# Where attention's projection tiles are read out of PSUM, one weight split further ahead, the first tokens in halves, and a last norm in three pieces

## The chip, the core and the metric

The kernel runs on one core of one Trainium2 chip. The core has a matrix engine (TensorE, PE in the profile), three engines for elementwise work (VectorE as DVE, ScalarE as ACT, GpSimd as POOL), and SyncE (SP), which here only issues transfers. Each engine runs its own instructions strictly in the order in which they were laid down; between engines they wait for each other by semaphores. Matmul results land in PSUM, everything else lives in SBUF, and inputs, weights and outputs are in HBM. The metric is the device time of one execution in microseconds (us), as the median of several runs.

## The reference, cut to what matters

One layer of a decoder for 512 prompt tokens and 64 sample tokens (8 requests of 8 tokens), all in float32, width 1024, 16 query heads of 64 in 4 groups, feed-forward width 2816:

```
h = x @ w_in                                  # u | v | q | k | attn v | gate_A | gate_B
u = gelu(u);  va = layer_norm(gelu(v))
y_A = u * (tril(W_s) va_chunk + b_s)          # chunks of 128 tokens
y_B = sliding window (128) attention with a position bias and one sink logit per head
mix = (sigmoid(g_a) * (y_A @ w_pa) + sigmoid(g_b) * (y_B @ w_pb)) @ w_o
x = layer_norm(alpha * x + mix)
x = layer_norm(alpha * x + (silu(x @ w_gate) * (x @ w_up)) @ w_down)
```

The outputs are both groups' x, the last 128 key and value rows of each, and the sample's normalised v.

## The kernel before

**Number format.** Every float32 operand of a matmul is split into a rounded part "hi" and a remainder "lo" (`split`: a ScalarE copy writes hi, a VectorE subtraction writes lo), and a product is three matmuls: hi·hi, hi·lo, lo·hi. This holds for the weights too. They come in units of 128x1024 numbers: `fetch` issues the transfer of a unit on SP's queue into one of 3 buffers ("raw"), `convert` splits it into one of 4 pairs of buffers ("hi", "lo", lines 114 and 115), and `unit(a, ahead=1)` hands out the next unit after it has made sure that the unit `ahead` places behind it has been split as well.

**Order.** The program is written once, in order. A planner lays down each engine's instructions before the run: among those that it takes to be ready, by its own estimate of times, it takes the one written first, and otherwise one written later. So an engine's order can differ from the written one, and buffers can be filled well ahead. `tc.issue_after(ins)` pins what a block writes for the engine of `ins` behind `ins` in that engine's order; for other engines it says nothing.

**The start.** Ten warming matmuls run on zeros. Meanwhile ScalarE's queue issues the transfer of the first eighth of x (feature block k = 0, `xT[:, 0]`), and SP's queue issues weight unit 0 in two halves, x for k = 1, two small bias inputs, x for k = 2 and 3, unit 1, x for k = 4 to 7, unit 2. In `projections_and_attention` a loop over the 8 feature blocks k splits x (576 tokens at once) and multiplies it with units 0 and 1 into two tiles ("ps").

**Attention.** There are 16 blocks, (group g, 128 tokens n). Block i has these steps, and TensorE has them in this order: `attention_turn` transposes the probabilities of block i ("pT"; ScalarE and VectorE split them into "pt", GpSimd masks them into "pc" and "pt"); `attention_values` multiplies those of block i - 1 with the values ("po"; ScalarE copies the lower half to "bot", VectorE adds it into yB); `attention_scores` makes the scores of block i + 2 ("sc"; then ScalarE's copy to "work", and on VectorE the mask at line 573, the bias at 575, the maximum at 579, two small operations at 582 and 583, then four exponentials on ScalarE at 585, and on VectorE the normalisation at 588 to 590); then `column_tile` fills TensorE's time with one tile of the projection w_in, 48 matmuls, in the order of `FILLS`: q3 u0 k1 q4 q5 u1 q6 q7 u2 ... u7 g0 g1. A finished tile is read out of PSUM by `evac_q` (ScalarE lines 491 and 494, VectorE 496 and 501), `evac_k` (ScalarE 471, VectorE 476, ScalarE 479) or, for u and g, by one ScalarE copy (line 813). For q and k tiles this is written in the next block, just before that block's scores; for u and g tiles at once after the matmuls. Scores and projection tiles share three PSUM buffers in turn, so that the scores of block i + 2 take the buffer of the projection tile of block i - 2. Instead of scores, block 14 has those of the sample tokens ("pss", softmax in "samS", lines 657 to 672); their probabilities are transposed ("pst", line 686) after the last block, in PSUM that the projection tiles give back.

**After attention** come the gMLP's v projection ("acc_v", eight weight units, the first four in a loop over n), gates, the merge, the output projection and the feed-forward. The kernel ends with `last_norm` on the last 128 tokens: VectorE's means, two small GpSimd operations for the reciprocal deviation r (`rstd`, lines 325 and 326), VectorE's first pass (z - mean) * g over 1024 columns (line 1341), and then z * r + b in three column ranges on VectorE, ScalarE and GpSimd, each sent out by its own transfer.

Of the kernel before, what the change touches and what calls it, by code (L numbers as in the profile page):

```python
# [11 lines left out]
F32 = mybir.dt.float32  # L12
# [3 lines left out]
ALU = mybir.AluOpType  # L16
AX = mybir.AxisListType

P = 128
D = 1024  # L20
KC = D // P
NP = 512
NS = 64
NT = NP + NS
HB = NT // 2
# [51 lines left out]
class Builder:  # L77
# [284 lines left out]
    def build(self):  # L362
        psum = lambda name, bufs: self.tc.tile_pool(
            name=name, bufs=bufs, space=bass.MemoryType.PSUM, reuse_waits="tile")
        with psum("pp0", 3) as self.pp, psum("pb0", 2) as self.pb:
            self.first_loads()
            self.constants()
            self.projections_and_attention()
        with psum("pb", 8) as self.pb:
            self.sample_first()  # L370
            self.gmlp()
            self.merge()
            self.output_projection()
            self.ffn()
            self.ffn_down()
# [19 lines left out]
        for _ in range(10):  # L395
            self.mm(ps, z[:, :P], z[:], True, True)

    def first_loads(self):
        self.xraw2 = [self.C([2, NT], F32, f"xraw{i}") for i in range(4)]
        self.nc.scalar.dma_start(out=self.xraw2[0][:, 0], in_=self.I["xT"][:, 0])  # L400
        self.fetch(0, parts=2)

    def load_x(self):
        nc, xT = self.nc, self.I["xT"]
        r = self.xraw2
        self.xraw = [r[k // 2][:, k % 2] for k in range(KC)]
        nc.sync.dma_start(out=r[0][:, 1], in_=xT[:, 1])
        self.bias_lookup()
        nc.sync.dma_start(out=r[1][:], in_=xT[:, 2:4])
        self.fetch(1)  # L410
        nc.sync.dma_start(out=r[2][:], in_=xT[:, 4:6])
        nc.sync.dma_start(out=r[3][:], in_=xT[:, 6:8])
        self.fetch(2)
# [138 lines left out]
    def attention_scores(self, g, n):  # L552


        nc = self.nc
        q0 = n * P
        sc = self.PS(f"sc{g}_{n}")
        for r in range(4):
            q = self.qs[2 * g + r // 2][:, r % 2, q0 : q0 + P]
            s = slice(q0 - P if n else 0, q0 + P if n else 2 * P)  # L560
            o = sc[:, r // 2, 256 * (r % 2) : 256 * (r % 2) + 256]
            self.mm(o, q, self.kt[g][:, 0, s], True, False)
            self.mm(o, q, self.kt[g][:, 1, s], False, True)
        scv = sc.rearrange("p b (h k) -> p (b h) k", h=2)
        work = self.R([2, 4, P], F32, f"work{g}_{n}")
        sel, pr = work[:, 0], work[:, 1]
        if n:
            nc.scalar.copy(out=sel, in_=scv[:, :, :P])
            cur = scv[:, :, P:]
        else:  # L570
            nc.gpsimd.memset(sel, NEG)
            cur = scv[:, :, :P]
        nc.vector.copy_predicated(
            out=sel, mask=self.cmask.unsqueeze(1).to_broadcast([P, 4, P]), data=cur)
        nc.vector.tensor_tensor(
            out=sel, in0=sel, in1=self.Bsel[g // 2][:, 4 * (g % 2) : 4 * (g % 2) + 4], op=ALU.add)
        st = self.ST(16, "att")
        nm, rs, es, rec = (st[:, 4 * i : 4 * i + 4] for i in range(4))
        nc.vector.tensor_reduce(out=nm, in_=sel, axis=AX.X, op=ALU.max, negate=True)
        sg = self.sinks[:, 4 * g : 4 * g + 4]  # L580
        nsg = self.nsinks[:, 4 * g : 4 * g + 4]
        nc.vector.tensor_tensor(out=nm, in0=nm, in1=nsg, op=ALU.min)  # L582
        nc.vector.tensor_tensor(out=es, in0=nm, in1=sg, op=ALU.add)
        for r in range(4):
            nc.scalar.activation(  # L585
                out=pr[:, r], in_=sel[:, r], func=AF.Exp, bias=nm[:, r : r + 1], accum_out=rs[:, r : r + 1])
        nc.scalar.activation(out=es, in_=es, func=AF.Exp)
        nc.vector.tensor_tensor(out=rs, in0=rs, in1=es, op=ALU.add)
        nc.vector.reciprocal(out=rec, in_=rs)
        nc.vector.tensor_tensor(  # L590
            out=pr, in0=pr, in1=rec.unsqueeze(2).to_broadcast([P, 4, P]), op=ALU.mult)
        return pr
# [21 lines left out]
    def attention_values(self, g, n, parts):  # L614
        nc = self.nc
        po = self.bank(f"po{g}_{n}")
        q0 = n * P
        mms = [(blk, m[:, i]) for m, blk in parts for i in range(2)]
        for j, (blk, m) in enumerate(mms):
            self.mm(po, self.av[blk // 2][:, blk % 2, g], m, j == 0, j == len(mms) - 1)  # L620
        bot = self.SG(f"bot{g}_{n}")
        nc.scalar.copy(out=bot[:HD, :512], in_=po[HD:])
        for i in range(2):
            f = lambda a: a.rearrange("p (c i q) -> p c i q", c=2, i=2)[:, :, i]
            nc.vector.tensor_tensor(
                out=self.yB[g][HD * i : HD * i + HD, :, q0 : q0 + P],
                in0=f(po[:HD]), in1=f(bot[:HD, :512]), op=ALU.add)
# [88 lines left out]
    def projections_and_attention(self):  # L716
# [11 lines left out]
        for k in range(KC):  # L728
            if k % 4 == 0:
                u = self.unit(4, parts=4, ahead=0)  # L730
            self.split(self.X[:, k, :NT], self.X[:, k, NT:], self.xraw[k])
            xh, xl = self.xact(k)
            for c in range(2):
                wh, wl = (w[:, k % 4, P * c : P * c + P] for w in u)
                for b in range(2):
                    s = slice(b * HB, (b + 1) * HB)
                    o = tiles[c][:, b, :HB]
                    self.mm(o, wh, xh[:, s], k == 0, False)
                    self.mm(o, wh, xl[:, s], False, False)
                    self.mm(o, wl, xh[:, s], False, k == KC - 1)  # L740
            if k == 1:
                self.bias_products()
# [17 lines left out]
        for i, (g, n) in enumerate(blocks):  # L760
            if n == 0:
                self.yB.append(self.C([2, NT], F32, f"yB{g}"))
            turned = self.attention_turn(g, n, probs[i])
            if i:
                with self.tc.issue_after(self.last_turned.ins):
                    self.attention_values(*waiting)
                self.run(fill)
            if i + 2 < len(blocks):
                probs.append(self.attention_scores(*blocks[i + 2]))
                if i + 4 == len(blocks):  # L770
                    with self.tc.issue_after(self.selected.ins):
                        kc, vc = self.sample_keys()
            elif i + 1 < len(blocks):
                S = self.sample_scores(kc)
            waiting = g, n, turned
            fill = self.column_tile(*fills[i])
            with self.tc.issue_after(self.copied.ins) if i + 2 == len(blocks) else nullcontext():
                next(fill, None)
            if i + 1 == len(blocks):
                with self.tc.issue_after(self.last_mm.ins):  # L780
                    self.attention_values(*waiting)
            next(fill, None)
            if fills[i][0] not in "qk":
                self.run(fill)
        self.run(fill)
        self.sample = S, vc
# [7 lines left out]
        for _ in gen:  # L794
            pass

    def column_tile(self, kind, c):

        ps = self.PS(f"ps{kind}{c}")
        u = self.unit(KC)  # L800
        self.fm(ps, u, self.xact, ks=range(7))
        yield
        self.fm(ps, u, self.xact, ks=range(7, KC))
        yield
        if kind == "k":
            self.evac_k(ps, c)
        elif kind == "q":
            self.evac_q(ps, c)
        else:
            tiles = self.u if kind == "u" else self.T  # L810
            if c % 2 == 0:
                tiles.append(self.C([2, NT], F32, f"{kind}{c}"))
            self.copied = self.nc.scalar.copy(
                out=tiles[c // 2][:, c % 2].rearrange("p (b c) -> p b c", b=2), in_=ps[:, :, :HB])
# [27 lines left out]
    def gmlp(self):  # L842
# [41 lines left out]
        norm = lambda t: self.norm_steps(st[t], v[t], rows[t], lng, lnb)  # L884
        acc = self.accumulators("v0")
        for n in range(4):
            u = {n: self.unit(2)}
            for t in range(NB + 1):
                tile(t, acc[t], u, (2 * n, 2 * n + 1))
            if n == 0:  # L890
# [443 lines left out]
    def last_norm(self, st, z, g, b, dst):  # L1334
# [3 lines left out]
        r = self.ST(1, "lnr")  # L1338
        nc.vector.bn_aggr(out=mv[:], in_=st.rearrange("p (a b) -> p a b", a=3))
        self.rstd(mv, r, P)  # L1340
        nc.vector.scalar_tensor_tensor(
            out=z[:], in0=z[:], scalar=mv[:, 0:1], in1=g[:], op0=ALU.subtract, op1=ALU.mult)
        c = slice(832, D)
        nc.scalar.activation(out=z[:, c], in_=z[:, c], func=AF.Copy, scale=r[:])
        nc.gpsimd.tensor_tensor(out=z[:, c], in0=z[:, c], in1=b[:, c], op=ALU.add)
        for k, queue in ((slice(0, 416), nc.scalar), (slice(416, 832), nc.sync)):
            nc.vector.scalar_tensor_tensor(
                out=z[:, k], in0=z[:, k], scalar=r[:], in1=b[:, k], op0=ALU.mult, op1=ALU.add)
            sent = queue.dma_start(out=dst[:, k], in_=z[:, k])
# [112 lines left out]
```

## Time and profile before

| | us |
|---|---|
| median of 3 runs | 891.38 (891.34 to 892.84) |
| the profiled execution, its own time | 893.83 |
| span of the profiled execution | 892.1 |
| TensorE's matmuls busy | 876.7 (98%) |
| VectorE busy | 630.5 (71%) |
| ScalarE busy | 404.0 (45%) |
| GpSimd busy | 193.0 (22%) |

The span runs from the first to the last recorded instruction or transfer of one execution; its own time has 1.7 us around that. Times in the trace count from the span's start. A busy time is the union of an engine's instructions; the ends of matmuls are modelled. "Idle before" is the time in which the engine stood still before an instruction, and the arrow names what ended it.

### The profile page before, as it was taken

The numbers are of one execution on the slowest core, as the hardware profiler recorded it, in microseconds if no ns is written. First come the engines' busy times: TensorE is split into PE (matmuls) and PEld (weight loads), VectorE is DVE, ScalarE is ACT, GpSimd is POOL, SyncE is SP. The second block draws the span as 40 slices with busy tenths as digits, with TensorE's granted clock in tenths as the row PEclk, the third lists the DMA queues.
The fourth block names the chain that finished last, engine by engine and source line by source line (L and its number), as shares of the span: only waits on it lengthen the run. The fifth ranks groups of instructions, "written<-read, shape, count | busy, mean of one in ns | idle before, by whom it ended". The sixth has DMA issues, their size and how long they took to land.

```text
span 892.1 us, 14718 instructions
## 1 busy us (share of the span) xinstructions
PE 876.7 (98%) x5911; PEld 822.5 (92%) x5911; DVE 630.5 (71%) x931; ACT 404.0 (45%) x767; POOL 193.0 (22%) x205
## 2 busy tenths in 40 slices
PE   8999999989999999999999999999999999999996
PEld 7999999978899999999988999999999998888885
DVE  5778887744789788867777777777777779224236
ACT  6556565573354446324342444444444457111110
POOL 3012214222332112233402222222222220000003
PEclk9999999989999999999999999999999999999999
DMA  9432124164123215233560022223222225322202
GB/s 326 125 98 71 49 62 153 44 200 126 46 71 117 95 48 186 93 117 107 175 229 24 1 72 95 95 96 95 95 96 95 95 95 189 96 71 95 71 4 103
DMA packets 31024, 91.85 MB, mean 103 GB/s; under 512 B 3947, under 2 KB 9100, under 8 KB 30924
## 3 DMA queue, kind: packets, MB, share of 16 engines
q1 hardware_dynamic: 30620, 88.45, 29.9%
q10 hardware_dynamic: 336, 2.47, 0.7%
q8 instruction: 46, 0.75, 0.3%
q14 instruction: 22, 0.18, 0.1%
HBM read 86.77 MB, written 6.10 MB: 104 GB/s over the span
## 4 chain that ended last, share of the span: by engine, by line
PE 88%; DVE 6%; ACT 3%; issue 1%; POOL 1%; DMA 0%; DVEq 0%; ACTq 0%; POOLq 0%
PE d L295 16%; PE xf L295 14%; PE zf L295 7%; PE acc_v L295 6%; PE acc_o L295 6%; PE pspa L295 6%; PE xg L295 5%; PE psu L295 4%; PE yf L295 4%; PE ffn L295 3%; PE zg L295 3%; PE xp L295 2%; PE psq L295 2%; PE psav L295 2%; PE ps L295 1%
## 5 line engine op out<-in xcount | busy, mean ns | idle before, releaser
L115 DVE TENSOR_TENSOR lo<-raw,hi 128x1024 fp32r<-128x1024 f32 (+1 forms) x78 | 90.4, 1169 | 99.5 <-ACT hi L114 99.1
L115 DVE TENSOR_TENSOR glo<-raw,ghi 128x1024 fp32r<-128x1024 f32 (+1 forms) x93 | 100.7, 1086 | 55.3 <-ACT ghi L114 55.3
L295 PE MATMUL d<-hi,h 128*128 128x512 f32 (+1 forms) x440 | 128.0, 368 | 0.0
L114 ACT CAST hi<-raw 128x1024 fp32r<-128x1024 f32 (+1 forms) x78 | 75.7, 985 | 109.6 <-PE d L295 82.6
L114 ACT CAST ghi<-raw 128x1024 fp32r<-128x1024 f32 (+1 forms) x93 | 83.4, 900 | 58.5 <-DVE raw L177 53.9
L295 PEld LDWEIGHTS d<-hi,h 128*128 128x128 f32 x440 | 79.9, 189 | 13.7
L295 PE MATMUL d<-lo,h 128*128 128x512 f32 (+1 forms) x242 | 89.6, 370 | 0.0
L177 POOL TENSOR_TENSOR raw<-raw,t 128x512 f32<-128x512 f32 x31 | 40.7, 1312 | 197.9 <-DVE glo L115 145.4
L177 POOL TENSOR_TENSOR t<-raw,raw 128x512 f32<-128x512 f32 x31 | 43.0, 1388 | 115.6 <-DVE raw L177 115.6
L295 PE MATMUL xf<-x1T,ghi 128*128 128x288 f32 x320 | 65.0, 295 | 0.0
L115 DVE TENSOR_TENSOR glo<-t,ghi 128x1024 fp32r<-128x1024 f32 x31 | 64.5, 2081 | 0.0
L295 PEld LDWEIGHTS d<-lo,h 128*128 128x128 f32 x242 | 45.6, 188 | 7.8
L295 PEld LDWEIGHTS xf<-x1T,ghi 128*128 128x128 f32 x320 | 51.4, 188 | 0.2 <-DVE u L226 0.2
L325 POOL TENSOR_SCALAR lnr<-lnmv 128x1 f32<-128x1 f32 (+1 forms) x15 | 14.2, 944 | 169.7 <-DVE lnmv L343 166.4
L295 PE MATMUL xf<-x1T,glo 128*128 128x288 f32 x160 | 47.1, 294 | 0.0
L295 PE MATMUL acc_o<-hi,m 128*128 128x512 f32 x144 | 46.3, 391 | 0.0
L295 PE MATMUL pspa<-yA,hi 128*128 128x288 f32 x256 | 44.6, 294 | 0.3 <-DVE yA L115 0.3
L585 ACT ACTIVATE work<-work,att 128x128 f32<-128x128 f32 x64 | 25.0, 392 | 43.1 <-DVE att L582 42.9
L295 PE MATMUL psu<-X,hi 128*128 128x288 f32 x256 | 44.1, 294 | 0.0
L609 POOL TENSOR_SCALAR_AFFINE_SELECT pc<-pt 128x512 fp32r<-128x512 f32 x24 | 16.6, 690 | 126.5 <-ACT pt L114 125.4
L295 PE MATMUL acc_v<-hi,X 128*128 128x512 f32 x128 | 42.9, 401 | 0.0
L295 PE MATMUL psq<-X,hi 128*128 128x288 f32 x224 | 38.8, 294 | 0.0
(366 smaller groups left out, 2478.7 us busy)
## 6 DMA issues: line engine op xcount, KB each, us to landing
raw<-in_wall_dram SPq DMA_DIRECT2D x133, 512.0 KB
xr<-in_xT_dram SPq DMA_DIRECT2D x8, 288.0 KB
z<-in_xtok_dram SPq DMA_DIRECT2D x4, 512.0 KB
xraw<-in_xT_dram SPq DMA_DIRECT2D x3, 576.0 KB
out_y_prompt_dram<-z SPq DMA_DIRECT2D x3, 512.0 KB
circ<-bout SPq DMA_DIRECT2D x1, 1024.0 KB
Bsel<-circ SPq DMA_DIRECT2D x2, 512.0 KB
kc<-in_kcT_dram SPq DMA_DIRECT2D x2, 512.0 KB
```

The lines of the kernel that those rows point to most:

```text
L114: self.nc.scalar.copy(out=hi, in_=src)
L115: return self.nc.vector.tensor_tensor(out=lo, in0=src, in1=hi.bitcast(F32), op=ALU.subtract)
L177: sub = lambda e, out, x, y: e.tensor_tensor(out=out, in0=x, in1=y, op=ALU.subtract)
L295: self.last_mm = self.nc.tensor.matmul(out, l, r, start=start, stop=stop, **more)
L325: self.nc.gpsimd.tensor_scalar_add(r[:n], mv[:n, 1:2], EPS)
L585: nc.scalar.activation(out=pr[:, r], in_=sel[:, r], func=AF.Exp, bias=nm[:, r : r + 1], accum_out=rs[:, r : r + 1])
L609: self.selected = nc.gpsimd.affine_select(out=f(out[:, i]), in_=f(pt[:, i].bitcast(F32)), pattern=[[0, 4], [sign, P]], compare_op=cmp, fil ...
```

## The change

Six edits. (a) The projection tile of block i - 1 is read out after the scores of block i + 2 are written, pinned on ScalarE behind this block's "bot" copy (`self.lower`, line 622) and on VectorE behind its line 583 (`self.shifted`). (b) The u and g tiles are read there too, except u7, which is still read at once. (c) In block 14 (tile g0) weights are split two units ahead and not one, and that split is no longer pinned behind u7's copy. (d) In the gMLP's first four steps ScalarE's part of the weight splits is pinned behind the last projection tile's copy (`self.copied`, here g1's). (e) At the start all loads go out on SP's queue, unit 0 in pieces of 256, 256 and 512 columns with x for k = 0 and k = 1 between them, and x for k = 0 is split in two halves of 288 tokens. (f) The last norm's first pass is done in three pieces of 192, 416 and 416 columns.

```
@@ build
-            self.first_loads()
@@ 
-    def first_loads(self):
-        self.xraw2 = [self.C([2, NT], F32, f"xraw{i}") for i in range(4)]
-        self.nc.scalar.dma_start(out=self.xraw2[0][:, 0], in_=self.I["xT"][:, 0])
-        self.fetch(0, parts=2)
-
     def load_x(self):
         nc, xT = self.nc, self.I["xT"]
-        r = self.xraw2
+        r = [self.C([2, NT], F32, f"xraw{i}") for i in range(4)]
         self.xraw = [r[k // 2][:, k % 2] for k in range(KC)]
-        nc.sync.dma_start(out=r[0][:, 1], in_=xT[:, 1])
+        raw = self.praw.tile([P, 1024], F32, tag="raw", name="raw0")
+        self.raws.append(raw)
+        for c0, c1, k in ((0, 256, 0), (256, 512, 1), (512, 1024, None)):
+            nc.sync.dma_start(out=raw[:, c0:c1], in_=self.I["wall"][0][:, c0:c1])
+            if k is not None:
+                nc.sync.dma_start(out=r[0][:, k], in_=xT[:, k])
         self.bias_lookup()
@@ attention_scores
-        nc.vector.tensor_tensor(out=es, in0=nm, in1=sg, op=ALU.add)
+        self.shifted = nc.vector.tensor_tensor(out=es, in0=nm, in1=sg, op=ALU.add)
@@ attention_values
-        nc.scalar.copy(out=bot[:HD, :512], in_=po[HD:])
+        self.lower = nc.scalar.copy(out=bot[:HD, :512], in_=po[HD:])
@@ projections_and_attention
-            self.split(self.X[:, k, :NT], self.X[:, k, NT:], self.xraw[k])
+            for t0, t1 in ((0, HB), (HB, NT)) if k == 0 else ((0, NT),):
+                self.split(self.X[:, k, t0:t1], self.X[:, k, NT + t0 : NT + t1], self.xraw[k][:, t0:t1])
...
                     self.attention_values(*waiting)
-                self.run(fill)
             if i + 2 < len(blocks):
                 probs.append(self.attention_scores(*blocks[i + 2]))
...
+            if i:
+                with self.tc.issue_after(self.lower.ins), self.tc.issue_after(self.shifted.ins):
+                    self.run(fill)
             waiting = g, n, turned
-            fill = self.column_tile(*fills[i])
-            with self.tc.issue_after(self.copied.ins) if i + 2 == len(blocks) else nullcontext():
-                next(fill, None)
+            before_last = i + 2 == len(blocks)
+            fill = self.column_tile(*fills[i], ahead=1 + before_last)
+            next(fill, None)
...
-            if fills[i][0] not in "qk":
+            if i + 3 == len(blocks):
                 self.run(fill)
@@ column_tile
-    def column_tile(self, kind, c):
+    def column_tile(self, kind, c, ahead=1):
-        u = self.unit(KC)
+        u = self.unit(KC, ahead=ahead)
@@ gmlp
         for n in range(4):
-            u = {n: self.unit(2)}
+            with self.tc.issue_after(self.copied.ins):
+                u = {n: self.unit(2)}
@@ last_norm
-        nc.vector.scalar_tensor_tensor(
-            out=z[:], in0=z[:], scalar=mv[:, 0:1], in1=g[:], op0=ALU.subtract, op1=ALU.mult)
-        c = slice(832, D)
+        c0, c1, c = slice(0, 416), slice(416, 832), slice(832, D)
+        for k in (c, c0, c1):
+            nc.vector.scalar_tensor_tensor(
+                out=z[:, k], in0=z[:, k], scalar=mv[:, 0:1], in1=g[:, k], op0=ALU.subtract, op1=ALU.mult)
...
-        for k, queue in ((slice(0, 416), nc.scalar), (slice(416, 832), nc.sync)):
+        for k, queue in ((c0, nc.scalar), (c1, nc.sync)):
```

## Rows read from the trace of the kernel before

**Rows 1.** The page's first part, the row of TensorE: PE is its matmuls, PEld its weight loads; busy time, share of the span, instructions.
```profile
PE 876.7 (98%) x5911; PEld 822.5 (92%) x5911; DVE 630.5 (71%) x931; ACT 404.0 (45%) x767; POOL 193.0 (22%) x205
```

**Rows 2.** Who TensorE's matmuls waited for over the whole span: total us, times, longest.
```profile
PE pst L686 <- ACT g L813: 1.6, 1, 1.6
...
PE sc L295 <- DVE Z L501: 1.5, 2, 1.0
...
PE po L295 <- POOL pt L609: 1.1, 1, 1.1
```

**Rows 3.** Busy time by stretch: the stretch and its length, then busy us and count of PE, PEld, DVE, ACT, POOL, then the granted clock as a share of full speed, the DMA share and GB/s.
```profile
120.00:140.00 20.00, 18.91 (x140) 17.99 (x139) 15.35 (x34) 13.87 (x43) 2.65 (x5) 1.00 0.25 77
...
190.00:195.00 5.00, 5.00 (x17) 4.29 (x18) 2.33 (x4) 4.96 (x6) 1.56 (x2) 0.50 0.85 209
```

**Rows 4.** TensorE's instructions in order of time around the end of attention: start, duration (of a merged group, from its first start to its last end), operation, output and inputs, shape, count, and in brackets the idle time before and what ended it.
```profile
184.56 0.76 PE L295 MATMUL po<-pc,av 128*128 128x512 f32 x2
...
187.31 0.69 PE L295 MATMUL psg<-X,hi 128*128 128x288 f32 x4
...
187.84 0.43 PE L295 MATMUL psg<-X,lo 128*128 128x288 f32 x2
...
189.84 1.97 PE L686 MATMUL pst<-ident,samS 128*128 128x128 f32 x8 [1.57 <-ACT g L813]
...
191.67 0.78 PE L295 MATMUL acc_v<-hi,X 128*128 128x512 f32 x1
...
196.00 0.62 PE L295 MATMUL acc_v<-hi,X 128*128 128x512 f32 x2
...
196.69 0.62 PE L295 MATMUL acc_v<-hi,X 128*128 128x512 f32 x2
```

**Rows 5.** VectorE, ScalarE and GpSimd in the same stretch, same columns.
```profile
176.86 1.22 DVE L115 TENSOR_TENSOR lo<-raw,hi 128x1024 fp32r<-128x1024 f32 x1
...
178.25 0.41 ACT L667 ACTIVATE samS<-samS,satt 128x136 f32<-128x136 f32 x1 [4.83 <-DVE satt L664]
...
164.12 1.22 POOL L609 TENSOR_SCALAR_AFFINE_SELECT pt<-pt 128x512 fp32r<-128x512 f32 x2
...
184.71 2.20 POOL L609 TENSOR_SCALAR_AFFINE_SELECT pt<-pt 128x512 fp32r<-128x512 f32 x2
...
184.84 1.58 DVE L115 TENSOR_TENSOR lo<-raw,hi 128x1024 fp32r<-128x1024 f32 x1
...
188.08 1.04 ACT L114 CAST hi<-raw 128x1024 fp32r<-128x1024 f32 x1
...
189.15 0.64 ACT L813 COPY g<-psg 128x576 f32<-128x576 f32 x1
```

**Rows 6.** TensorE and VectorE inside attention, same columns.
```profile
53.43 0.74 DVE L573 COPY_PREDICATED work<-misc,sc 128x512 f32<-128x512 int32 x1
...
55.84 0.16 DVE L583 TENSOR_TENSOR att<-att,misc 128x4 f32<-128x4 f32 x1
...
78.73 3.06 DVE L476 TENSOR_TENSOR kt<-psk,kt 64x576 fp32r<-64x576 f32 x4 [0.34 <-ACT kt L471]
...
82.63 1.10 PE L295 MATMUL sc<-kt,qs 128*128 128x256 f32 x8
...
89.35 1.52 DVE L496 SCALAR_TENSOR_TENSOR qs<-psq,qs 64x576 fp32r<-64x576 f32 x2 [0.48 <-ACT Z L494]
...
126.83 1.19 PE L295 MATMUL sc<-kt,qs 128*128 128x256 f32 x8 [1.04 <-DVE Z L501]
...
135.10 0.94 PE L295 MATMUL po<-pt,av 128*128 128x512 f32 x2
```

**Rows 7.** The start of the kernel. Instructions in order of time; the first row is a transfer's issue on SP's queue.
```profile
3.12 0.36 SPq L409 DMA_DIRECT2D xraw<-in_xT_dram  x1
...
5.80 0.53 PE L295 MATMUL ps<-X,hi 128*128 128x288 f32 x2 [0.75 <-ACT X L114]
...
6.60 0.40 PE L295 MATMUL ps<-X,hi 128*128 128x288 f32 x1 [0.27 <-DVE X L115]
...
8.47 1.25 ACT L114 CAST X<-xraw 128x576 fp32r<-128x576 f32 x2 [1.53 <-DMA xraw<-in_xT_dram]
...
12.70 2.75 DVE L115 TENSOR_TENSOR X<-xraw,X 128x576 fp32r<-128x576 f32 x4
...
13.73 0.56 PE L295 MATMUL ps<-X,hi 128*128 128x288 f32 x3
```

**Rows 8.** VectorE and GpSimd in two norms, same columns: the first three rows are from the norm after the output projection, the last four from the norm that ends the kernel.
```profile
494.31 1.31 POOL L325 TENSOR_SCALAR lnr<-lnmv 128x1 f32<-128x1 f32 x1 [1.05 <-DVE lnmv L343]
...
495.40 1.27 DVE L348 SCALAR_TENSOR_TENSOR z<-z,lnmv,ln1g 128x1024 f32<-128x1024 f32 x1
...
495.70 1.40 POOL L326 TENSOR_TENSOR lnr<-lnr,mhalf 128x1 f32<-128x1 f32 x1
...
885.19 1.28 DVE L1341 SCALAR_TENSOR_TENSOR z<-z,lnmv,ln 128x1024 f32<-128x1024 f32 x1
...
885.24 1.31 POOL L325 TENSOR_SCALAR lnr<-lnmv 128x1 f32<-128x1 f32 x1 [3.28 <-DVE lnmv L1339]
...
886.64 0.57 POOL L326 TENSOR_TENSOR lnr<-lnr,mhalf 128x1 f32<-128x1 f32 x1
...
887.24 1.56 DVE L1347 SCALAR_TENSOR_TENSOR z<-z,lnr,ln 128x416 f32<-128x416 f32 x2 [0.77 <-POOL lnr L326]
```


## The prediction, made before the changed kernel ran

> **What bounds the kernel now.** Read the page's first part first: TensorE's matmuls are busy 98% of the span [rows 1]. So only about 15 us (892.1 - 876.7) can be gained without taking matmuls away, and the change takes none away: what counts is where TensorE stands still, or runs slowly while it is called busy. The list of its waits is the second view. Of its long rows three lie in attention and behind it: 1.6 us before the transposes of the sample's probabilities, behind the ScalarE copy of tile g1; 1.5 us in two waits of scores for VectorE's reading of a q tile; 1.1 us of a value product for GpSimd's masks [rows 2]. The third view, busy time by stretch, shows what the list can't: from 190 to 195 us TensorE is busy all the time, but at a granted clock of 0.50, the lower of its two levels (1.2 against 2.4 GHz) [rows 3]. Two pauses stand just before it, 1.07 us (in the wait for the masks) and 1.57 us, within 4 us. A single pause of 1.04 us at 126.8 us left the stretch around it at 1.00 [rows 3, 6]. So attention's end costs more than its waits. Two more places are without matmuls: the start, with 0.75 and 0.27 us of waits for the first tokens [rows 7], and the last norm, where nothing but the norm runs [rows 8].
>
> **The end of attention, edits (b), (c) and (d).** Four value matmuls of block 15 stand from 184.56 to 187.31 us, 2.75 us, where matmuls of that shape need 0.23 each (three in 196.69 - 196.00 = 0.69) [rows 4]: 2.75 - 0.92 = 1.83 us lost. They wait for GpSimd's two last masks, which end at 184.71 + 2.20 = 186.91 and take 1.22 us elsewhere; VectorE split weights at 184.84, 1.58 us, beside them [rows 5]. The masks are late because VectorE split two more weight units while the sample's softmax waited for it: ScalarE stood idle 4.83 us before the exponentials at 178.25, and 1.22 us of it is the split at 176.86 [rows 5]. Counted by buffers, that split is the gMLP's second unit and the one at 184.84 its third. Edit (d) pins ScalarE's half of both behind g1's copy, so VectorE's half goes too: 1.22 us before the softmax and 0.98 us in the masks (2.20 - 1.22), 2.2 us together. The last mask then ends near 184.7, and the last of the four matmuls would start at 184.56 + 0.69 = 185.25: the pause is gone. Edit (c) lets two further splits run earlier, which only adds slack. I take 1.8 us; if only the 1.22 us come through, 186.91 - 1.22 = 185.69 leaves 0.44 of it, so 1.4 at least.
>
> The second pause: g1's last matmuls are over at 187.84 + 0.43 = 188.27, but ScalarE splits a weight unit from 188.08 and copies g1 only at 189.15 [rows 4, 5]. Edit (d) forbids just this order. The copy starts at about 188.3: 0.85 us gained (0.9 at most; 0 if another ScalarE instruction takes the place). A pause of 1.57 - 0.85 = 0.7 us is left, the copy's own length.
>
> The clock: with one pause of 0.7 us, less than the 1.04 that cost nothing, I expect it to stay up. From 189.84 to 195 us 5.2 us of matmuls ran at half rate; at the full rate the same work takes half: 2.6 us gained, or nothing if it falls all the same.
>
> What is late next: the gMLP's later units are now split after 188.3 us. The second is needed only after the first unit's 28 matmuls (6.4 us at 0.23) and the sample's value products, so some 10 us are there for a ScalarE copy of 1.04 and a VectorE subtraction of 1.22. Free.
>
> **Inside attention, edit (a).** VectorE has from mask to line 583 an unbroken 53.43 to 56.00 = 2.6 us and then nothing to do while ScalarE makes exponentials; reading a q tile takes it 1.5 us and a little more [rows 6]. The edit puts the score steps ahead of the reading, which then fills the pause. It should end the two waits of scores (1.5 us) and the 0.3 us by which a value pair at 135.10 is too long (0.94 against 0.62) [rows 2, 4, 6]: 1.8 us, the most it can give. It has a price: the buffer is read out later, and the scores of the next block but one want that buffer. Queued behind the pinned reading on VectorE are the normalisation and, behind its end, those scores. For q tiles TensorE's 8.6 us per block leave room once VectorE keeps up. For the k tile, 3.06 us on VectorE, they don't: it ended at 81.79, the scores used its buffer at 82.63 [rows 6]. Moved behind 2.6 us of score steps it ends at 84.4, less about 0.9 for the waits that the old order made (0.34 before it, and the lower-half copy that stood behind two of its ScalarE copies): 83.5, so scores late by 0.9 us. Without those 0.9 it is 1.8, and 3.0 with a weight split of 1.2 in front; 0.5 is the least. With 0.3 for the first q tile I take +1.2 new and -1.8 old: 0.6 gained, between 1.3 gained and 1.5 lost. Edit (b) takes a copy off ScalarE's way to the next "pt"; TensorE isn't waiting there, so nothing.
>
> **The start, edit (e).** The first product can't gain more than its two waits, 1.0 us. That it keeps them is doubtful: tokens k = 2 and 3 are waited for until 8.47, 5.3 us after their issue at 3.12, behind the bytes ahead of them, which stay the same; and VectorE, busy from then on, has k = 4's remainder ready at about 12.70 + 0.7 = 13.4, while TensorE comes to k = 4 at 13.73 [rows 7]. So at most 0.4 us survive. The two issues moved onto SP (0.4 us each) come ahead of k = 2's, hidden in those 5.3 us; if not, 0.8 us late makes 0.4 lost. I take 0.3.
>
> **The last norm, edit (f).** GpSimd's first small operation runs 1.31 us, as long as VectorE's pass beside it (1.28), and ends 0.08 behind it [rows 8]. In the earlier norm it ended at 495.62, right after one pass and inside the next, and the second operation then ran 1.40 us and ended 0.43 behind the next pass (495.40 + 1.27) [rows 8]. So each waits for a whole VectorE instruction but slips in between two. With pieces of about 0.4, 0.6 and 0.6 us: first operation done at 885.7, second when the second piece ends (886.2) plus 0.43 = 886.6; the pieces end at 886.8, where the second pass starts instead of 887.24. I take 0.45 us. If GpSimd gets in only after the last piece: 886.75 + 0.43 = 887.2, nothing.
>
> The Trainium skill (SBUF — State Buffer, Who interferes with whom) says that VectorE with two SBUF inputs and a GpSimd instruction that reads SBUF exclude each other for a whole instruction, by order of issue. The trace agrees on whole instructions; taken strictly, the second operation, issued behind a running piece, could lose to every next one, and the term would be 0 instead of 0.45.
>
> **The sum.** 1.8 + 0.85 + 2.6 + 0.6 + 0.3 + 0.45 = 6.6 us. It is made against the profiled execution (893.83, 1.7 outside its span), which stands 2.45 above the median and 1.0 above the highest run; I take it off the median: 891.38 - 6.6 = 884.8.
>
> **Rivals.**
> 1. The clock falls anyway: a pause of 0.7 us, thin work around it. For it: the fall came in a pause, and I have one example of a harmless one. 6.6 - 2.6 = 4.0: 887.4.
> 2. The masks stay late: the planner puts other splits where the removed ones were. For it: VectorE is full there. Pause, clock and all: 0.85 + 0.6 + 0.3 + 0.45, and half a us of the first pause: 2.7, 888.7.
> 3. Nothing lasts: later stages are tied to something that doesn't move, transfers or the splits now after 188.3, or the clock drops elsewhere. Against it: TensorE's list shows no long wait after 190 us. 0 to 1.5 gained: about 890.6.
> 4. Slower: reading behind the score steps makes every q and k tile's buffer late. The six tiles must cost the 6.0 us of the other terms plus the 1.8 that (a) removes, 7.8: from 1.3 us of wait per tile on, the kernel is slower. At 1.8 each: 10.8 - 7.8 = 3.0, 894.4. For it: the k tile's 0.9 to 3.0. Against: a q tile needs 1.5 us in a pause of about 1.7.
> That the edits do nothing is part of 3.
>
> **How the numbers follow.** The forecast 0.60, rival 1 0.14, rival 2 0.10, rival 3 0.10, rival 4 0.06. The first three are faster by over 0.2% (1.8 us, about what this kernel's runs can tell): 0.84; rival 3 within it: 0.10; slower 0.06. The forecast's own range: the best ends add 0.7 inside attention, 0.1 at the start and 0.1 elsewhere (883.9), the worst take 2.1 off attention (886.9). Below it I add 0.5, a third of the spread of the three runs; above, rivals 1 and 2 reach 888.7. So 883.4 to 888.8 holds 0.84.
>
> **What would show it.** After: no wait of "po" for GpSimd above 0.4 us and none of "pst" above 0.9; a granted clock of 1.00 from about 183 to 190 us; scores waiting about 1 us behind line 479 or 476 near 83 us, and none near 91 and 127; k = 4's first matmul 0.3 us earlier; line 326 ending 0.5 us sooner after line 1339. Wrong if the clock row shows 0.50 there, if scores wait in most blocks up to 127 us, or if new waits of "acc_v" stand behind 190 us.

## The result, and the profile after

The changed kernel takes 887.54 us (median of 5 runs, 886.80 to 887.83) where the kernel before takes 892.84 on the same chip (5 runs, 891.34 to 894.15): a ratio of 0.9943, interval 0.9929 to 0.9958, or 5.3 us less. Between the two profiled executions the span falls by 6.3 us (892.1 to 885.8). The prediction was 884.8: 6.6 us off a median of 891.38.

TensorE's part of the page and the whole list of what its matmuls waited for, after; they answer to [rows 1, 2].

```profile
PE 873.7 (99%) x5911; PEld 821.0 (93%) x5911; DVE 630.7 (71%) x934; ACT 405.8 (46%) x769; POOL 195.5 (22%) x205
```
```profile
PE warm L295 <- DVE zero L392: 1.3, 1, 1.3
PE pst L685 <- ACT g L815: 0.7, 1, 0.7
PE ps L295 <- DVE X L115: 0.7, 2, 0.4
PE psq L295 <- ACT misc L478: 0.5, 1, 0.5
PE ps L295 <- ACT X L114: 0.5, 1, 0.5
PE pspa L295 <- DVE yA L115: 0.3, 1, 0.3
```

The waits of "po" and of "sc" are gone, "pst" has halved, and one of "psq" is new. Busy time fell by 3.0 us although no matmul was taken away: matmuls that ran at the lower clock counted as busy. The windows answer to [rows 3]: the granted clock is 1.00 in all three, the middle one begins just after the pause before pst.

```profile
120.00:140.00 20.00, 20.00 (x153) 19.74 (x152) 17.64 (x34) 11.70 (x33) 6.83 (x9) 1.00 0.28 78
187.00:189.00 2.00, 2.00 (x15) 1.79 (x14) 1.32 (x2) 2.00 (x4) 2.00 (x2) 1.00 0.08 7
190.00:195.00 5.00, 5.00 (x25) 3.60 (x23) 3.50 (x6) 4.97 (x6) 2.49 (x1) 1.00 1.02 357
```

A list of waits shows where TensorE stood, not how far it got. For that, take the same matmul in both traces and subtract its start times. The change of this shift between two such places is what the stretch between them gained or lost.

| matmul | before | after | shift | this stretch | predicted |
|---|---|---|---|---|---|
| first of tile "psq" | 20.12 | 21.28 | +1.16 | **+1.16** | -0.3 |
| scores behind the value pair of [rows 6] | 135.88 | 135.48 | -0.40 | **-1.56** | -0.6 |
| last psg group, behind the masked products | 187.31 | 185.09 | -2.22 | **-1.82** | -1.8 |
| pst | 189.84 | 186.76 | -3.08 | **-0.86** | -0.85 |
| first of "pso" | 199.98 | 194.26 | -5.72 | **-2.64** | -2.6 |
| last of the kernel | 883.68 | 877.91 | -5.77 | -0.05 | 0 |
| end of the span | 892.1 | 885.8 | -6.3 | **-0.5** | -0.45 |

Four terms came out within 0.1 us. Two are wrong and cancel in part: the start lost 1.16 where 0.3 was to be gained, and the inside of attention gained 1.56 where 0.6 was predicted.

The end of attention, in TensorE's order of time; it answers to [rows 4], and the GpSimd row to [rows 5].

```profile
184.63 0.62 PE L295 MATMUL po<-pt,av 128*128 128x512 f32 x2
185.09 0.69 PE L295 MATMUL psg<-X,hi 128*128 128x288 f32 x4
186.76 1.09 PE L685 MATMUL pst<-ident,samS 128*128 128x128 f32 x8 [0.73 <-ACT g L815]
```
```profile
180.74 1.22 POOL L608 TENSOR_SCALAR_AFFINE_SELECT pt<-pt 128x512 fp32r<-128x512 f32 x2
```

The last masks end at 181.96, more than 2.5 us before their product. The pause before pst is 0.73, and the eight transposes take 1.09 us where they took 1.97 at the lower clock.

Inside attention: the long score wait of [rows 6] (126.83, 1.04 us) is now none, the value pair takes 0.62 and not 0.94, and the k tile, read by VectorE behind the score steps, holds up a projection tile.

```profile
84.27 0.76 DVE L475 TENSOR_TENSOR kt<-psk,kt 64x576 fp32r<-64x576 f32 x1
```
```profile
85.44 0.80 PE L295 MATMUL psq<-X,hi 128*128 128x288 f32 x4 [0.55 <-ACT misc L478]
126.82 1.12 PE L295 MATMUL sc<-kt,qs 128*128 128x256 f32 x8
135.02 0.62 PE L295 MATMUL po<-pt,av 128*128 128x512 f32 x2
```

The start answers to [rows 7]. TensorE begins without a wait and 0.7 us sooner (5.80 before), but ScalarE gets tokens k = 2 and 3 at 10.04 and not at 8.47, and k = 4 begins at 14.60 and not at 13.73.

```profile
5.07 0.77 PE L295 MATMUL ps<-X,hi 128*128 128x288 f32 x2
10.77 0.53 PE L295 MATMUL ps<-X,hi 128*128 128x288 f32 x2 [0.54 <-ACT X L114]
14.60 0.85 PE L295 MATMUL ps<-X,hi 128*128 128x288 f32 x3
```
```profile
10.04 1.25 ACT L114 CAST X<-xraw 128x576 fp32r<-128x576 f32 x2 [2.09 <-DMA xraw<-in_xT_dram]
```

The last norm answers to [rows 8]: VectorE's three pieces and its second pass, and GpSimd's two small operations beside them.

```profile
879.41 1.54 DVE L1346 SCALAR_TENSOR_TENSOR z<-z,lnmv,ln 128x192 f32<-128x192 f32 x3
880.87 1.55 DVE L1351 SCALAR_TENSOR_TENSOR z<-z,lnr,ln 128x416 f32<-128x416 f32 x2
```
```profile
879.47 0.45 POOL L325 TENSOR_SCALAR lnr<-lnmv 128x1 f32<-128x1 f32 x1 [3.28 <-DVE lnmv L1342]
880.00 0.82 POOL L326 TENSOR_TENSOR lnr<-lnr,mhalf 128x1 f32<-128x1 f32 x1
```

The second small operation ends at 880.82, while the pieces still run (to 880.95), so the second pass follows them at once.

### The profile page after: what moved, and what is told of

The parts are those of the page before. It is cut to its first block, busy times and chain, and to the rows that moved or that the text cites. A ratio compares the mean times of both kernels' runs of the same rounds, so it can differ in the third digit from the quotient of the medians.

```text
span 885.8 us, 14732 instructions
## 1 busy us (share of the span) xinstructions
PE 873.7 (99%) x5911; PEld 821.0 (93%) x5911; DVE 630.7 (71%) x934; ACT 405.8 (46%) x769; POOL 195.5 (22%) x205
## 4 chain that ended last, share of the span: by engine, by line
PE 92%; DVE 4%; ACT 1%; issue 1%; DMA 1%; SPq 0%; POOL 0%; DVEq 0%; ACTq 0%; POOLq 0%
PE d L295 16%; PE xf L295 14%; PE zf L295 7%; PE acc_v L295 6%; PE acc_o L295 6%; PE pspa L295 6%; PE xg L295 5%; PE psu L295 5%; PE yf L295 4%; PE psq L295 3%; PE ffn L295 3%; PE zg L295 3%; PE xp L295 2%; PE psav L295 2%; PE psg L295 1%; PE yg L295 1%
## 5 line engine op out<-in xcount | busy, mean ns | idle before, releaser
L325 POOL TENSOR_SCALAR lnr<-lnmv 128x1 f32<-128x1 f32 (+1 forms) x15 | 12.3, 821 | 168.8 <-DVE lnmv L343 165.5
L608 POOL TENSOR_SCALAR_AFFINE_SELECT pc<-pt 128x512 fp32r<-128x512 f32 x24 | 23.1, 962 | 110.9 <-ACT pt L114 109.2
```

The source lines that it names most:

```text
L325: self.nc.gpsimd.tensor_scalar_add(r[:n], mv[:n, 1:2], EPS)
L608: self.selected = nc.gpsimd.affine_select(out=f(out[:, i]), in_=f(pt[:, i].bitcast(F32)), pattern=[[0, 4], [sign, P]], compare_op=cmp, fil ...
```

## The experiments

Twelve kernels, each against the kernel before on the same chip (its median was 892.6 to 893.0 each time). Differences to the changed kernel's 887.54 go across chips. Between all of them the traces are compared by the shift of the same matmul, as above.

**The start.** *e_undone* puts the old start back into the changed kernel: x for k = 0 on ScalarE's queue, unit 0 in halves.

```
     def build(self):
...
+            self.first_loads()
...
-            for t0, t1 in ((0, HB), (HB, NT)) if k == 0 else ((0, NT),):
-                self.split(self.X[:, k, t0:t1], self.X[:, k, NT + t0 : NT + t1], self.xraw[k][:, t0:t1])
+            self.split(self.X[:, k, :NT], self.X[:, k, NT:], self.xraw[k])
```

> The changed kernel with the start of the kernel before: x for k = 0 on ScalarE's queue, unit 0 in two halves, x for k = 0 split whole. Theory 1 (the start is slower by 1.16 us, where the first matmul of psq stands at 21.28 against 20.12, and nothing later takes that up): 887.5 - 1.2 = 886.3, with that first psq matmul near 20.1. Theory 2 (the 1.16 us at the start are spare, because attention's first blocks wait for something else anyway): 887.5, with the psq matmul early and a new wait before 80 us.

886.50 us (886.35 to 886.62). The first psq matmul is back at its old place (20.18, before 20.12), 1.10 us ahead of the changed kernel's, and so are the transposes at pst; at the last matmul it is still 0.80. So the loss at the start is real, and most of it reaches the end. What makes it? *bias_act* takes the two additional issues out of the way of tokens k = 2 and 3.

```
-        nc.sync.dma_start(out=rb[:NBKT], in_=self.I["rel_bias"])
-        nc.sync.dma_start(out=self.sel, in_=self.I["bias_sel"])
+        nc.scalar.dma_start(out=rb[:NBKT], in_=self.I["rel_bias"])
+        nc.scalar.dma_start(out=self.sel, in_=self.I["bias_sel"])
```

> The changed kernel, with the two small bias inputs issued on ScalarE's queue in place of SP's. x for k = 2 and 3 is then issued sixth on SP's queue, near 3.1 us as in the kernel before, while unit 0 still comes in pieces of 256 columns. Theory 'issues' (x for k = 2 and 3 is late by the two issues that were put ahead of it): ScalarE begins to split it near 8.5 and not 10.04, the first psq matmul stands at 20.1 or a little before, 886.2. Theory 'rows' (the pieces of 256 columns move in rows of 1 KB and take the transfer engines longer): no change at 10.04, 887.5.

887.40 us (886.97 to 887.57). The issue on SP's queue and ScalarE's split of what it brings:

```profile
3.13 0.43 SPq L408 DMA_DIRECT2D xraw<-in_xT_dram  x1
```
```profile
9.98 1.25 ACT L114 CAST X<-xraw 128x576 fp32r<-128x576 f32 x2 [0.81 <-DMA xraw<-in_xT_dram]
```

Issued as early as in the kernel before (3.12), it lands as late as in the changed one. The issues aren't the cause. *unit_halves* keeps all loads on SP's queue and brings unit 0 in two pieces of 512 columns.

```
-        for c0, c1, k in ((0, 256, 0), (256, 512, 1), (512, 1024, None)):
+        for c0, c1, k in ((0, 512, 0), (512, 1024, 1)):
...
```

> The changed kernel, with unit 0 in two pieces of 512 columns (rows of 2 KB, as in the kernel before) and not three, still all on SP's queue, x for k = 0 behind the first and x for k = 1 behind the second. x for k = 2 and 3 is then issued seventh, one place earlier. Theory 'issues': half of the loss comes back, ScalarE splits it near 9.3, first psq matmul near 20.7, 887.0. Theory 'rows': all of it, near 8.5 and 20.1, 886.4.

886.05 us (885.66 to 886.74).

```profile
3.59 0.36 SPq L407 DMA_DIRECT2D xraw<-in_xT_dram  x1
```
```profile
7.96 1.25 ACT L114 CAST X<-xraw 128x576 fp32r<-128x576 f32 x2 [1.22 <-DMA xraw<-in_xT_dram]
```

Issued 0.46 later than in *bias_act*, it is split 2.0 us earlier, and the four runs (885.66 to 886.74) lie below the four of *bias_act* on the same chip. So the pieces of 256 columns cost the start, and neither the one queue nor the halves of x do. *short_long* asks whether it is their number or their short rows.

```
-        for c0, c1, k in ((0, 256, 0), (256, 512, 1), (512, 1024, None)):
+        for c0, c1, k in ((0, 256, 0), (256, 1024, 1)):
```

> The changed kernel, with unit 0 in two pieces of 256 and 768 columns, all on SP's queue, x for k = 0 and k = 1 behind them. Theory 'count' (each further transfer ahead of x for k = 2 and 3 costs about one transfer's time, however small): landing as with two halves, ScalarE splits it near 8.0, first psq matmul near 19.7, 886.1. Theory 'rows' (rows of 1 KB are slow in themselves): half of the loss, near 9.0, first psq matmul near 20.5, 886.8.

886.39 us (886.23 to 887.08), with the split at 9.45 and the first psq matmul at 20.70. The positions are those of "rows", the time lies between, and the landing varies: at the same start as *unit_halves*, *best_a* below has it at 9.12. Over all kernels of this case it is 8.1 to 8.5 with the old start (four of them), 9.3 to 10.2 with pieces of 256, 256 and 512 columns on SP's queue (six), and 8.0 and 9.1 with halves there. The last two ranges all but touch, so the verdict on the pieces rests on the medians (887.5 and 887.4 with them, 886.1 and 885.7 with halves). Whether their number or their row length makes them slow stays open. *two_queues* (x for k = 0 and the bias inputs on ScalarE's queue, the three pieces kept) didn't test what it was made for: the planner put unit 1 ahead of tokens k = 2 and 3.

> The changed kernel, with x for k = 0 and the two bias inputs on ScalarE's queue and unit 0 in its three pieces, x for k = 1 and then x for k = 2 and 3 on SP's. x for k = 2 and 3 is issued fifth, near 2.7 us. Theory 'issues': ScalarE splits it near 8.0, earlier than in either kernel, first psq matmul at 19.6 to 19.9, so 886.0 or a little less. Theory 'rows': it stays near 10, 887.5. If instead the bytes ahead of it set its landing, as the prediction had it, it lands at 8.5 whatever the issue, 886.3.

887.97 us (887.47 to 888.05), the slowest of the five. Those tokens were issued at 4.26 only, and the first piece of unit 0, now beside another queue's transfer, was split at 4.26 and not at 2.98. That the other queue is the cause isn't shown: the second piece also follows the first more closely here.

**The end of attention.** *d_alone* is the kernel before with the pin behind g1's copy and nothing else.

```
         for n in range(4):
-            u = {n: self.unit(2)}
+            with self.tc.issue_after(self.copied.ins):
+                u = {n: self.unit(2)}
```

> The kernel before with edit (d) alone. ScalarE's order loses the split ahead of the sample's exponentials and the two ahead of g1's copy. If (d) alone carries the end of attention, as the prediction's sum has it: no wait of po for GpSimd (1.8), pst's pause at 0.7 (0.85), clock at 1.00 (2.6), 5.3 us less than the kernel before: near 887 where before stands at 892.5. If edits (b) and (c) are needed to free VectorE and ScalarE in time for the masks: half of the first pause stays, 0.9 us, and the clock may fall with it: 888 to 891.

888.38 us (888.21 to 888.62), 4.4 under before's median and 5.5 by the spans. The shifts are -1.90 before psg, -0.86 more at pst, -2.64 more at pso: the three terms of the prediction, from edit (d) alone. GpSimd's last masks begin at 183.63 and take 1.22 us, so they end at 184.85 (184.7 predicted).

```profile
183.63 1.22 POOL L609 TENSOR_SCALAR_AFFINE_SELECT pt<-pt 128x512 fp32r<-128x512 f32 x2
```

*d_undone* takes that pin out of the changed kernel.

> The changed kernel without edit (d): the splits of the gMLP's first four units are no longer pinned behind g1's copy. In ScalarE's order one of them stands ahead of g1's copy again, and one each ahead of u7's copy and behind the sample's exponentials. The pause before pst should be near 1.6 us again (+0.9). What else comes depends on the masks and the clock. Theory 'one pause is enough': the clock falls to 0.50 behind the 1.6 us alone, +2.6, 891.0 in all, and 892.8 if the masks are late as well. Theory 'two pauses': if the masks are in time, so that the 1.6 us stand alone, the clock stays at 1.00 and the kernel takes 888.4.

888.52 us (887.67 to 889.04), 1.0 above the changed kernel. The masks stay in time (shift -2.06 at psg): the other edits free them as well, so (d) and they are two ways to the same 1.8 us. Which of them does it isn't shown; (a) to (c) are the ones that touch attention. The pause before pst is back, and alone it leaves the clock up; the other three executions have the same mean clock as this one, 0.998.

```profile
187.75 1.09 PE L685 MATMUL pst<-ident,samS 128*128 128x128 f32 x8 [1.56 <-ACT g L815]
```
```profile
187.00:189.00 2.00, 1.25 (x10) 1.24 (x11) 1.22 (x1) 1.96 (x3) 1.32 (x2) 1.00 0.33 130
189.00:191.00 2.00, 2.00 (x10) 1.63 (x9) 1.22 (x3) 1.99 (x3) 0.71 (x1) 1.00 0.62 203
```

*first_pause* is the reverse: the kernel before with the pin for the fourth unit only (`if n > 1`), so that the masks stay late and only pst's pause shrinks.

> The kernel before, with only the gMLP's fourth unit's split (and so the one ahead of g1's copy) pinned behind g1's copy: the splits beside the sample's softmax stay. The masks stay late, so the 1.8 us before psg stay, and pst's pause falls from 1.6 to 0.7. Theory 'both pauses': the clock fell for the two together, and with one of them cut to 0.7 us it stays at 1.00: -0.85 - 2.6 = 3.5 less, near 889 where before stands at 892.5. Theory 'the first pause': the masks' pause alone brings the fall, the clock still shows 0.50, 0.85 less, 891.8.

891.09 us (890.77 to 892.77). The profiled execution is one of three that took 892.3 to 892.8 us at a granted clock of 0.995, as a mean over the whole execution. The other seven took 890.8 to 891.2 at 0.997 or 0.998, which is what kernels without a fall show.

```profile
187.11 0.51 PE L295 MATMUL po<-pt,av 128*128 128x512 f32 x1 [1.07 <-POOL pt L609]
189.14 1.97 PE L686 MATMUL pst<-ident,samS 128*128 128x128 f32 x8 [0.73 <-ACT g L813]
```
```profile
187.00:189.00 2.00, 1.29 (x7) 1.02 (x7) 0.77 (x3) 1.14 (x3) 0.06 (x1) 0.91 0.58 152
189.00:191.00 2.00, 1.86 (x10) 1.83 (x10) 1.11 (x2) 1.61 (x3) 0.00 (x0) 0.50 1.00 399
191.00:193.00 2.00, 2.00 (x9) 1.62 (x8) 1.72 (x3) 1.84 (x2) 1.69 (x2) 0.74 0.37 49
```

The same view of the kernel before, around its fall:

```profile
187.00:189.00 2.00, 1.26 (x7) 0.98 (x7) 0.81 (x2) 1.44 (x2) 0.00 (x0) 0.89 0.59 188
195.00:197.00 2.00, 2.00 (x10) 1.60 (x9) 0.00 (x0) 2.00 (x3) 0.32 (x1) 0.90 0.82 266
```

In this execution of *first_pause* the clock falls behind 1.07 and 0.73 us of recorded idle, though each is shorter than the 1.56 that did no harm alone. But 1.07 is only a part of the first pause: the four value products take 2.65 us (184.80 to 187.45) for 0.92 us of work, so TensorE stood 1.7 us there and 2.5 in both pauses. The clock comes back by 192 us (0.26 x 2 / 0.5 = 1.0 us of the third window are at half rate), after 3.4 us; in the kernel before it is down from 188.6 to about 195.4, for 6.8 us. Does the place decide, or how much TensorE stood? *one_long_pause* copies tile g1 four times in the changed kernel, so that one pause stands behind full work.

```
-            self.copied = self.nc.scalar.copy(
...
+            for _ in range(4 if (kind, c) == ("g", 1) else 1):
+                self.copied = self.nc.scalar.copy(
...
```

> The changed kernel, with tile g1's copy done four times over into the same place (three copies of 0.6 us too many, same result), so that TensorE stands before pst in one pause of 0.73 + 3 x 0.6 = 2.5 us with full work ahead of it. That is more than the two pauses of 1.07 and 0.73 us together, behind which the clock fell. Theory 'sum' (so much standing in a few us brings the fall, however it is cut): the clock shows 0.50 behind it, +1.8 and +1.3 to 2.6, 890.6 to 892. Theory 'the masks' (the fall belongs to what TensorE does around the masks, with little done between 185 and 189 us): the clock stays at 1.00, 889.3.

889.84 us (888.83 to 891.18), between the two forecasts. The profiled execution took 890.95 at a mean clock of 0.996; four of the ten, 888.8 to 889.7, have 0.998.

```profile
188.70 1.30 PE L685 MATMUL pst<-ident,samS 128*128 128x128 f32 x8 [2.74 <-ACT g L816]
```
```profile
189.00:191.00 2.00, 2.00 (x12) 1.77 (x11) 1.38 (x2) 2.00 (x4) 0.00 (x0) 0.61 0.01 4
191.00:193.00 2.00, 2.00 (x7) 1.58 (x6) 2.00 (x2) 1.98 (x3) 0.00 (x0) 0.54 0.88 248
```

Here it falls behind a single pause too, with the masks in time: late masks aren't needed for it. By the mean clocks it doesn't fall in every execution. From pst to pso this trace loses 1.6 us against the changed kernel (the shift goes from -3.08 to -5.72 there, from -1.14 to -2.19 here), beside the 1.9 of the pause itself.

**Inside attention.** *ab_undone* reads each projection tile before the scores again (u and g tiles at once), with everything else as changed.

```
                     self.attention_values(*waiting)
+                self.run(fill)
...
-            if i:
-                with self.tc.issue_after(self.lower.ins), self.tc.issue_after(self.shifted.ins):
-                    self.run(fill)
...
-            if i + 3 == len(blocks):
+            if fills[i][0] not in "qk":
                 self.run(fill)
```

> The changed kernel with edits (a) and (b) undone: a projection tile is read out of PSUM before the scores again, u and g tiles at once. By the positions of TensorE's matmuls in the two traces, (a) and (b) are worth 1.56 us between 20 and 136 us (the waits of scores near 91 and 127 and a long pair of value products at 135): 887.5 + 1.6 = 889.1, with sc waiting for Z of a q tile twice, 0.5 and 1.0 us, and the end of attention as in the changed kernel. By the prediction's own term it is 0.6: 888.1.

889.06 us (888.53 to 889.94), 1.5 above the changed kernel, as the positions said. Both score waits are back:

```profile
91.88 1.19 PE L295 MATMUL sc<-kt,qs 128*128 128x256 f32 x8 [0.46 <-DVE Z L500]
127.32 1.19 PE L295 MATMUL sc<-kt,qs 128*128 128x256 f32 x8 [1.08 <-DVE Z L500]
```

*k_early* reads only the k tile before the scores.

```
                     self.attention_values(*waiting)
+                if fills[i - 1][0] == "k":
+                    self.run(fill)
```

> The changed kernel, but the k tile is read out before the scores, as in the kernel before; q and u tiles stay as changed. Theory 'k tile': the 0.55 us by which psq waits at 85.44 for the k tile's last copy is gone, and the 0.7 us that TensorE falls behind there: 886.8. Theory 'passed on': reading it first pushes that block's score steps back by 3 us on VectorE, and the loss comes as a wait of the next transposes or scores: 887.5 or more.

887.29 us (886.96 to 887.57), no different from 887.54. The wait at 85.44 is gone and a longer one stands one tile later; it is made good only at pst (shift -1.43 at psg, -3.17 at pst), which has no wait of its own there.

```profile
94.27 0.77 PE L295 MATMUL psu<-X,hi 128*128 128x288 f32 x4 [1.43 <-DVE Z L500]
```

**A faster version.** *best_a* takes *unit_halves* and moves one copy of the k tile.

```
         for i in range(2):
...
                 nc.scalar.copy(out=f(self.kt[2 * c + i][64 * o : 64 * o + 64, 0]), in_=ps[s, :, :HB])
+        nc.scalar.copy(out=self.kraw[:, c, :], in_=ps[:, 1, HB - 192 : HB])
...
-        nc.scalar.copy(out=self.kraw[:, c, :], in_=ps[:, 1, HB - 192 : HB])
```

> The changed kernel with unit 0 in two halves (886.05 us when it ran alone) and, in the reading of a k tile, ScalarE's copy of the last 192 keys ahead of VectorE's remainders in place of behind them. The buffer is then free with VectorE's last remainder: the wait of psq for the k tile shortens by 0.3 us, 885.7. If VectorE's end sets it together with that copy's place ahead of the exponentials, nothing is gained, 886.0.

885.65 us (885.43 to 886.50, 5 runs), ratio to before 0.9929, interval 0.9916 to 0.9941: the fastest here, 1.9 under the changed kernel. psq now waits 0.29 us, for VectorE. That the copy helps shows in this row; against *unit_halves* the 0.4 us are inside the spread.

```profile
84.25 0.77 PE L295 MATMUL psq<-X,hi 128*128 128x288 f32 x4 [0.29 <-DVE kt L475]
```

## Why the prediction was right or wrong

**The forecast as a whole.** Its mechanism and its sign held; the sum was 6.6 where the spans give 6.3, with two wrong terms that cancel in part. But 887.54 lies 2.7 above 884.8 and outside the forecast's own 883.9 to 886.9. It is inside the stated range only by the room left for rivals 1 and 2, and by the time alone it would be rival 1's 887.4; the clock rows tell the two apart. The step that was off is "I take it off the median". The sum was read from an execution in which the clock fell, and taken off a median that has the time of executions in which it seems not to have fallen.

Each execution's mean granted clock is on record. It includes a few us at 0.50 behind the last matmul (in the kernel before, 889 to 892 us), so it is under 1.00 in all. Of the 44 executions of the kernel before that ran beside the twelve kernels, 17 took 891.2 to 891.6 us at 0.997, 19 took 892.4 to 893.5 at 0.995 or 0.996, and 8 took 893.8 to 894.4 at 0.994 or 0.995. The changed kernel's five have 0.997 or 0.998. The profiled execution (893.83, 0.994) is of the last group, and the base, 891.38, has a time of the first. Without the clock's 2.6 the sum is 4.0, and 891.38 - 4.0 = 887.4.

**First pause, 1.8: 1.82 measured.** The route was right (*d_alone*: masks at 184.85). What the step missed is that the other edits free the masks as well, (c) or reading tiles later being the likely ones. In the changed kernel they end at 181.96, and taking (d) out costs none of this term.

**Second pause, 0.85: 0.86.** This one is edit (d)'s, as argued (*d_undone*).

**The clock, 2.6: 2.64 between the two profiled executions.** "I expect it to stay up" held, and rival 1 falls. Over executions it is worth less: the medians of the three groups of the kernel before are 891.4, 892.9 and 894.1, so a lower mean clock goes with 1.6 or 2.7 us more, and 17 of 44 executions seem to have no fall. This fits the 1.0 us by which the spans (6.3) fall further than the medians (5.3). In the traces the fall came with 1.07 + 0.73, with 1.07 + 1.57 and with 2.74 alone, not with 1.04, 0.73 or 1.56 alone (recorded idle). Where the border lies isn't shown. Rival 2 (masks stay late) and rival 3 (nothing lasts) fall with the table: from pso to the last matmul the shift changes by 0.05.

**Inside attention, 0.6: 1.56.** Two sizes were off. The new cost was 0.73 and not 1.2: the k tile ended at 85.03, which is 83.87 without the start's 1.16 and so inside the prediction's 83.5 to 84.4, but it wasn't the scores that wanted its buffer. The step "the scores of the next block but one want that buffer" took the turn of the three buffers from the old order. With the reading written behind the scores, it is the block's projection tile that waits for it (85.44, for line 478), behind the scores, which are 1.1 us long and wait for nothing. The first q tile made no wait (0.3 predicted). And the old waits were worth more than their rows: 1.04 idle gave a shift of 1.28, 0.46 gave 0.62, the long pair 0.39 for 0.32. Rival 4 needed 1.3 us per tile; one tile of six cost 0.7.

**The start, 0.3 gained: 1.16 lost** in the profile, 1.0 by the medians of *e_undone*. The step that failed is not the moved issues, which are hidden as it said (*bias_act*, *unit_halves*), but "behind the bytes ahead of them, which stay the same". The bytes did, their transfers didn't. The Trainium skill (DMA: Bandwidth & Descriptors, Why a DMA increments its semaphore by 16 and not by 1) names, in its column for the previous generations, 2 KiB per partition as the minimum transfer that saturates the DMAs. Pieces of 256 columns are 1 KB per partition. The times of this case go the same way, with 887.5 for such pieces and 886.1 for pieces twice as long; *short_long*, at 886.4 with one short piece, doesn't settle whether the length is the reason. The first product did keep its 0.7 us, and lost them at k = 2, as the prediction feared.

**The last norm, 0.45: 0.52.** From the last matmul's start to the end of the span takes 8.39 to 8.40 us in the three profiled kernels without (f) and 7.78 to 7.88 in the eleven with it. GpSimd slipped in between two pieces, as read from the earlier norm. The strict reading of the Trainium skill (SBUF — State Buffer, Who interferes with whom), by which it could have lost to every next piece, would have given 0; the row 880.00, 0.82 speaks against that here.

## What to carry to other kernels

Sum a change by the shift of the same matmul in two traces, not by the list of waits: errors of opposite sign show, and so does the clock. Where the matrix engine stands twice in short order, look at the clock behind it: in the profiled execution it was worth more (2.6 us) than either pause (1.8, 0.9). Before a sum from a trace is taken off a median, look whether the profiled execution is like the median's: here it had a lower mean clock (0.994, where executions of the median's time have 0.997) and was 2.45 us longer. When a first load is cut to come sooner, look at what is queued behind it; pieces of half a unit cost nothing against the old start, pieces of a quarter cost 1.2 us by the first psq matmul.

## What was not expected of the hardware

A wait's recorded idle time understates what it costs by 0.16 to 0.24 us (0.46, 0.55 and 1.04 us of idle are shifts of 0.62, 0.73 and 1.28), 0.16 of it since the modelled end of the matmul ahead of it lies late. Four matmuls of 128x288 take 0.69 us together and 0.29 each by the rows, so they follow each other every 0.13, and the recorded end of one lies 0.16 behind the start of a next one that doesn't wait.

One and the same kernel kept the clock in some executions and, by its mean, lost it in others (17 and 27 of 44 for the kernel before). In the traces it stayed low for 3.4 us in two and 6.8 in another. Kernels whose clock fell there spread more from run to run (2.0 to 3.2 us over 10 to 15 runs) than the others (at most 1.4 us over 4 to 6), and the times go by the mean clock; where in an unprofiled execution the clock was low isn't on record.
